# Rotary embedding: whole input resident on chip, loads queued first, 16 KB runs per partition, and a sine table in fewer steps

## The chip, the cores and the metric

The kernel runs on one core of a Trainium2 chip. The metric is device time in microseconds (us) of one execution. VectorE is called DVE, ScalarE ACT, GpSimd POOL and SyncE SP, as in the profile. The 16 DMA engines of the core move data between HBM and the on-chip memory (128 partitions). A DMA is issued by one of the engines' queues; those of POOL make one queue of their own (q0 in the profile), those of SP and ACT another kind (q1).

## The reference

`x` has 8 x 8 heads of 1024 positions with 64 features in f32 (16.8 MB); the output has the same shape and type. Each half of the features is rotated against the other by an angle that depends on the position and the feature:

```python
angles = np.outer(positions, freqs)          # 1024 x 32
cos, sin = np.cos(angles), np.sin(angles)
x_first, x_second = x[..., :half], x[..., half:]
out_first = x_first * cos - x_second * sin
out_second = x_first * sin + x_second * cos
```

## The kernel before

The positions are split over the 128 partitions: a partition owns 8 neighbouring positions (Q = 8) of every head. The sine and cosine tables are then 8 x 32 = 256 values per partition and serve all heads; they are repeated over the heads by a broadcast pattern.

The program first loads the frequencies (line 39, on POOL's queue) and the positions (line 44, on SP's), multiplies them (line 49) and adds a quarter turn for the cosine (line 52). Each of the two angle arrays is then reduced twice to one turn, on DVE (lines 58 to 65: scale, round by conversion to int32 and back, scale, subtract), ACT takes the sine of it (line 66), and DVE turns the result into bf16 (lines 71, 72).

The main loop (line 80) has eight tiles of K = 8 heads. A tile is a load from f32 in HBM to bf16 on chip (line 87), six bf16 operations on DVE with 2048 elements per partition each (lines 96 to 101: two products with the sine, two with the cosine, a difference, a sum), and a store from bf16 to f32 (line 102). Loads and stores are all issued by POOL, since they convert the type on the way. In HBM, a partition's part of one head is 512 floats, 2 KB in one run; a tile has eight such runs per partition, one per head, and neighbouring partitions lie 2 KB apart.

Input, output and the two temporaries t1 and t2 come from a pool of four buffers per name. A load of tile 4 or later therefore waits until DVE has read tile t - 4. Program order on each engine is laid down by the framework, which may put instructions of several tiles between one another; each engine works through its own instructions in order, and waits on semaphores for the others.

Of the kernel before, what the change touches and what calls it, by code (L numbers as in the profile page):

```python
# [2 lines left out]

# [4 lines left out]


@with_exitstack
def kernel(
    ctx: ExitStack,
    tc: tile.TileContext,
    x: bass.AP,
    freqs: bass.AP,
    positions: bass.AP,
    out: bass.AP,
):
    nc = tc.nc  # L20
    Sin = mybir.ActivationFunctionType.Sin

    b, h, seq, d = x.shape
    bh = b * h
    half = d // 2
    P = 128
    twopi = 2 * math.pi

    ss = d
    sbh = seq * d  # L30
    Q = seq // P
    assert Q * P == seq

    singles = ctx.enter_context(tc.tile_pool(name="singles", bufs=1))
    cspool = ctx.enter_context(tc.tile_pool(name="cs", bufs=1))
    pool = ctx.enter_context(tc.tile_pool(name="main", bufs=4))

    fr = singles.tile([P, 1, half], mybir.dt.float32)
    nc.gpsimd.dma_start(out=fr, in_=freqs[None, None, :].to_broadcast([P, 1, half]))  # L39

    pos_i = singles.tile([P, Q, 1], positions.dtype)
    pos_ap = bass.AP(tensor=positions.tensor, offset=positions.offset,
                     ap=[[Q, P], [1, Q], [1, 1]])
    nc.sync.dma_start(out=pos_i, in_=pos_ap)
    pos_f = singles.tile([P, Q, 1], mybir.dt.float32)
    nc.vector.tensor_copy(out=pos_f, in_=pos_i.bitcast(mybir.dt.int32)[:, :, :1])  # L46

    angles = cspool.tile([P, Q, half], mybir.dt.float32)
    nc.vector.tensor_mul(out=angles, in0=pos_f.to_broadcast([P, Q, half]),  # L49
                         in1=fr.to_broadcast([P, Q, half]))  # L50
    anglesc = cspool.tile([P, Q, half], mybir.dt.float32)
    nc.vector.tensor_scalar_add(out=anglesc, in0=angles, scalar1=math.pi / 2)
    sin_p = cspool.tile([P, 1, Q, half], mybir.dt.float32)
    cos_p = cspool.tile([P, 1, Q, half], mybir.dt.float32)
    for a, dst in ((angles, sin_p), (anglesc, cos_p)):
        for shift in (0.0, math.pi):
            if shift:
                nc.vector.tensor_scalar_add(out=a, in0=a, scalar1=shift)  # L58
            bfrac = cspool.tile([P, Q, half], mybir.dt.float32)
            nc.vector.tensor_scalar_mul(out=bfrac, in0=a, scalar1=1.0 / twopi)  # L60
            bint = cspool.tile([P, Q, half], mybir.dt.int32)
            nc.vector.tensor_copy(out=bint, in_=bfrac)  # L62
            nc.vector.tensor_copy(out=bfrac, in_=bint)  # L63
            nc.vector.tensor_scalar_mul(out=bfrac, in0=bfrac, scalar1=twopi)  # L64
            nc.vector.tensor_sub(out=a, in0=a, in1=bfrac)  # L65
        nc.scalar.activation(out=dst[:, 0, :, :], in_=a, func=Sin, scale=-1.0)  # L66

    bf16 = mybir.dt.bfloat16
    sin_h = cspool.tile([P, 1, Q, half], bf16)
    cos_h = cspool.tile([P, 1, Q, half], bf16)  # L70
    nc.vector.tensor_copy(out=sin_h, in_=sin_p)
    nc.vector.tensor_copy(out=cos_h, in_=cos_p)  # L72

    K = 8
    ntiles = bh // K
    sin_b = sin_h.to_broadcast([P, K, Q, half])
    cos_b = cos_h.to_broadcast([P, K, Q, half])
    sp = Q * ss

    for t in range(ntiles):  # L80
        g0 = t * K
        x_ap = bass.AP(tensor=x.tensor, offset=x.offset + g0 * sbh,
                       ap=[[sp, P], [sbh, K], [ss, Q], [1, d]])
        o_ap = bass.AP(tensor=out.tensor, offset=out.offset + g0 * sbh,
                       ap=[[sp, P], [sbh, K], [ss, Q], [1, d]])
        xt = pool.tile([P, K, Q, d], bf16)
        nc.gpsimd.dma_start(out=xt, in_=x_ap)  # L87
        ot = pool.tile([P, K, Q, d], bf16)
        of = ot[:, :, :, :half]
        os_ = ot[:, :, :, half:]  # L90
        t1 = pool.tile([P, K, Q, half], bf16)
        t2 = pool.tile([P, K, Q, half], bf16)
        xf = xt[:, :, :, :half]
        xs = xt[:, :, :, half:]
        v = nc.vector
        v.tensor_mul(out=t1, in0=xf, in1=sin_b)  # L96
        v.tensor_mul(out=t2, in0=xs, in1=sin_b)  # L97
        v.tensor_mul(out=of, in0=xf, in1=cos_b)  # L98
        v.tensor_sub(out=of, in0=of, in1=t2)  # L99
        v.tensor_mul(out=os_, in0=xs, in1=cos_b)  # L100
        v.tensor_add(out=os_, in0=os_, in1=t1)  # L101
        nc.gpsimd.dma_start(out=o_ap, in_=ot)  # L102


# [1 line left out]
_INS = ['x', 'freqs', 'positions']  # L106
_OUTS = [((8, 8, 1024, 64), 'float32')]


# [23 lines left out]
```

## Time and profile before

| | us |
|---|---|
| median of 3 runs (100.31 to 100.55) | 100.53 |
| span of the profiled execution, first to last instruction | 98.8 |
| what the median has beside that span | 1.73 |
| DVE busy | 62.8 |
| POOL busy, nearly all of it issuing DMAs | 15.0 |
| ACT busy | 2.1 |
| TensorE | not used |

The whole time of the profiled execution is not listed apart from its span, so the span stands for it and the third row of the table links it to the runs. In the profile's rows, `L96 DVE ... t<-xt,sin_h` is line 96 on DVE, writing t from xt and sin_h; what stands in brackets at the end of a row of the timeline is the time for which the engine stood idle before it, and what released it. In the groups by line, the two figures after the bar are the busy time of the group in us and the mean of one in ns. The engines' busy time in a DMA row can be over 1.00 of a stretch, because recorded packets of one DMA engine overlap. The rate in GB/s counts what a transfer writes: a load writes bf16, a store writes f32.

### The profile page before, as it was taken

To read this page: it belongs to the slowest core of one execution; us is meant where nothing else is said; L and a number is where in the kernel's file an instruction comes from. 1 tells how busy PE (TensorE), PEld (TensorE's weight loads), DVE (VectorE), ACT (ScalarE), POOL (GpSimd) and SP (SyncE) were. 2 spreads that over 40 slices of the span, in tenths; PEclk is the share of its full clock that TensorE was granted. 3 is DMA by queue.
4 is the path that set the end of the run, shared out by engine and by line. 5 is a ranking of instruction groups with operands and counts; after the bars stand their busy time and mean duration, and the time that the engine had idled before them with its cause. 6 is when DMAs were issued, how large, how long until landed. Compare 5 with 4: busy or idle time off the path is not lost.

```text
span 98.8 us, 150 instructions
## 1 busy us (share of the span) xinstructions
DVE 62.8 (64%) x75; ACT 2.1 (2%) x3; POOL 15.0 (15%) x21
## 2 busy tenths in 40 slices
DVE  0179973746999999999993000001999999991000
ACT  5000100010000000000000000000000000000000
POOL 5920000000033030302004900000002003003000
DMA  0699999999808999999999999999999997994992
GB/s 3 40 97 189 203 209 206 208 206 206 136 4 101 180 201 417 418 417 412 418 416 413 415 417 365 251 206 207 208 207 208 297 423 202 352 378 122 392 382 73
DMA packets 16817, 25.20 MB, mean 255 GB/s; under 512 B 416, under 2 KB 8624, under 8 KB 16816
## 3 DMA queue, kind: packets, MB, share of 16 engines
q0 software_dynamic: 16672, 25.18, 116.3%
q1 hardware_dynamic: 144, 0.01, 0.1%
q14 instruction: 1, 0.01, 0.0%
HBM read 16.80 MB, written 16.78 MB: 340 GB/s over the span
## 4 chain that ended last, share of the span: by engine, by line
issue 33%; DVE 30%; DMA 19%; POOL 7%; POOLq 1%; PEldq 0%
DMA xt<-in_x_dram 19%; DVE ot L101 6%; DVE ot L100 6%; DVE ot L99 6%; DVE ot L98 6%; POOL xt L87 4%; DVE t L96 4%; DVE t L97 3%; POOL out_dram L102 3%; POOLq L128 1%; POOL fr L39 1%; DVE cos_h L72 0%; POOLq L102 0%; PEldq L128 0%
## 5 line engine op out<-in xcount | busy, mean ns | idle before, releaser
L96 DVE TENSOR_TENSOR t<-xt,sin_h 128x2048 bf16<-128x2048 bf16 x8 | 9.8, 1220 | 20.9 <-DMA xt<-in_x_dram 20.9
L102 POOL DMA_DIRECT2D out_dram<-ot x8 | 7.1, 883 | 52.0 <-DVE ot L101 52.0
L87 POOL DMA_DIRECT2D xt<-in_x_dram x8 | 7.1, 898 | 22.6 <-DVE ot L100 22.6
L97 DVE TENSOR_TENSOR t<-xt,sin_h 128x2048 bf16<-128x2048 bf16 x8 | 9.7, 1217 | 0.0
L100 DVE TENSOR_TENSOR ot<-xt,cos_h 128x2048 bf16<-128x2048 bf16 x8 | 9.7, 1216 | 0.0
L98 DVE TENSOR_TENSOR ot<-xt,cos_h 128x2048 bf16<-128x2048 bf16 x8 | 9.7, 1216 | 0.0
L99 DVE TENSOR_TENSOR ot<-ot,t 128x2048 bf16<-128x2048 bf16 x8 | 9.7, 1215 | 0.0
L101 DVE TENSOR_TENSOR ot<-ot,t 128x2048 bf16<-128x2048 bf16 x8 | 9.7, 1215 | 0.0
L46 DVE CAST pos_f<-pos_i 128x8 f32<-128x8 int32 x1 | 0.4, 369 | 2.5 <-DMA pos_i<-in_positions_dram 2.5
L49 DVE TENSOR_TENSOR angles<-pos_f,fr 128x256 f32<-128x256 f32 x1 | 0.4, 424 | 2.4 <-DMA fr<-in_freqs_dram 2.4
L66 ACT ACT_TABLE_LOAD x1 | 1.3, 1283 | 0.7 <-PEq L117 0.7
L64 DVE TENSOR_SCALAR bfrac<-bfrac 128x256 f32<-128x256 f32 x4 | 1.2, 292 | 0.1
L62 DVE CAST bint<-bfrac 128x256 int32<-128x256 f32 x4 | 1.2, 292 | 0.1
L63 DVE CAST bfrac<-bint 128x256 f32<-128x256 int32 x4 | 1.2, 292 | 0.1
L65 DVE TENSOR_TENSOR angles<-angles,bfrac 128x256 f32<-128x256 f32 x2 | 0.8, 425 | 0.1
L65 DVE TENSOR_TENSOR anglesc<-anglesc,bfrac 128x256 f32<-128x256 f32 x2 | 0.8, 420 | 0.0
L39 POOL DMA_DIRECT2D fr<-in_freqs_dram x1 | 0.7, 706 | 0.8 <-PEq L128 0.8
L66 ACT ACTIVATE cos_p<-anglesc 128x256 f32<-128x256 f32 x1 | 0.4, 416 | 10.6 <-DVE anglesc L65 10.6
L60 DVE TENSOR_SCALAR bfrac<-anglesc 128x256 f32<-128x256 f32 x2 | 0.6, 290 | 0.0
L60 DVE TENSOR_SCALAR bfrac<-angles 128x256 f32<-128x256 f32 x2 | 0.6, 289 | 0.0
L66 ACT ACTIVATE sin_p<-angles 128x256 f32<-128x256 f32 x1 | 0.4, 416 | 7.8 <-DVE angles L65 7.8
L58 DVE TENSOR_SCALAR anglesc<-anglesc 128x256 f32<-128x256 f32 x1 | 0.3, 294 | 0.0
(8 smaller groups left out, 1.6 us busy)
## 6 DMA issues: line engine op xcount, KB each, us to landing
out_dram<-ot POOLq DMA_DIRECT2D x8, 2048.0 KB, 11.4
xt<-in_x_dram POOLq DMA_DIRECT2D x8, 1024.0 KB, 17.0
pos_i<-in_positions_dram SPq DMA_DIRECT2D x1, 8.0 KB, 1.8
fr<-in_freqs_dram POOLq DMA_DIRECT2D x1, 16.0 KB, 3.9
```

The source lines that it names most:

```text
L39: nc.gpsimd.dma_start(out=fr, in_=freqs[None, None, :].to_broadcast([P, 1, half]))
L60: nc.vector.tensor_scalar_mul(out=bfrac, in0=a, scalar1=1.0 / twopi)
L65: nc.vector.tensor_sub(out=a, in0=a, in1=bfrac)
L66: nc.scalar.activation(out=dst[:, 0, :, :], in_=a, func=Sin, scale=-1.0)
L87: nc.gpsimd.dma_start(out=xt, in_=x_ap)
L96: v.tensor_mul(out=t1, in0=xf, in1=sin_b)
L97: v.tensor_mul(out=t2, in0=xs, in1=sin_b)
L98: v.tensor_mul(out=of, in0=xf, in1=cos_b)
L99: v.tensor_sub(out=of, in0=of, in1=t2)
L100: v.tensor_mul(out=os_, in0=xs, in1=cos_b)
L101: v.tensor_add(out=os_, in0=os_, in1=t1)
L102: nc.gpsimd.dma_start(out=o_ap, in_=ot)
```

## The change

A partition now owns 64 neighbouring positions (C = 64) of one head: 16 partitions cover a head (`chunks`), a tile is 8 heads (`group`), and a tile in HBM is one unbroken piece of 2 MB in which each partition has one run of 64 x 64 floats, 16 KB. There are again eight tiles, and the six operations on each have the same sizes as before. The table is now 64 x 32 = 2048 values per partition, the same values in every 16th partition, without a broadcast over heads.

Input and output tiles have eight buffers each, so none is used twice; the temporaries have two. All eight loads stand in the program ahead of the table's computation. The positions are loaded by eight small DMAs, alternately from SP and ACT; the frequencies follow on ACT.

The table is computed in turns instead of radians: frequency divided by a full turn, product with the positions, rounding to whole turns by adding and subtracting a large constant in one instruction, one subtraction. ACT takes the sine of the remaining fraction and, for the cosine, the sine of a quarter turn less its absolute value, writing bf16 directly.

```diff
-    pool = ctx.enter_context(tc.tile_pool(name="main", bufs=4))
+    xpool = ctx.enter_context(tc.tile_pool(name="xin", bufs=ntiles))
+    opool = ctx.enter_context(tc.tile_pool(name="xout", bufs=ntiles))
+    tpool = ctx.enter_context(tc.tile_pool(name="tmp", bufs=2))
-    nc.gpsimd.dma_start(out=fr, in_=freqs[None, None, :].to_broadcast([P, 1, half]))
-    nc.sync.dma_start(out=pos_i, in_=pos_ap)
+    def hbm(t, g):
+        return bass.AP(tensor=t.tensor, offset=t.offset + g * P * run, ap=[[run, P], [1, run]])
+    for g in range(group):
+        eng = nc.sync if g % 2 == 0 else nc.scalar
+        eng.dma_start(
+            out=pos_i[g * chunks:(g + 1) * chunks],
...
+    nc.scalar.dma_start(out=fr, in_=freqs[None, :].to_broadcast([P, half]))
+    for g in range(ntiles):
+        xt = xpool.tile([P, C, d], bf16)
+        nc.gpsimd.dma_start(out=xt.rearrange("p c d -> p (c d)"), in_=hbm(x, g))
+        xts.append(xt)
...
+    nc.vector.tensor_scalar_mul(out=fturn[:, 0, :], in0=fr, scalar1=1.0 / twopi)
+    nc.vector.tensor_mul(out=turns, in0=pos_f.to_broadcast([P, C, half]),
+                         in1=fturn.to_broadcast([P, C, half]))
+    nc.vector.tensor_scalar(out=whole, in0=turns, scalar1=magic, scalar2=magic,
+                            op0=Alu.add, op1=Alu.subtract)
+    nc.vector.tensor_sub(out=turns, in0=turns, in1=whole)
+    nc.scalar.activation(out=sin_h, in_=turns, func=Sin, scale=twopi)
+    nc.scalar.activation(out=whole, in_=turns, func=mybir.ActivationFunctionType.Abs)
+    nc.scalar.activation(out=cos_h, in_=whole, func=Sin, scale=-twopi, bias=half_pi)
...
-        xt = pool.tile([P, K, Q, d], bf16)
-        nc.gpsimd.dma_start(out=xt, in_=x_ap)
-        nc.gpsimd.dma_start(out=o_ap, in_=ot)
+        nc.gpsimd.dma_start(out=hbm(out, g), in_=ot.rearrange("p c d -> p (c d)"))
```

On POOL, the whole queue of DMAs before, from the frequencies to the last store, in program order (xt is an input tile, ot an output tile):

```order
L39 DMA fr<-in_freqs_dram 128x32
L87 DMA xt<-in_x_dram 128x8x512 x5
L102 DMA out_dram<-ot 128x8x512 x5
L87 DMA xt<-in_x_dram 128x8x512 x3
L102 DMA out_dram<-ot 128x8x512 x3
```

And the same place on POOL now, from the end of the program's preamble:

```order
L118 MEMSET const-bfloat16-1.0 128x1
L118 MEMSET const-uint8-127 128x1
L129 UNCONDITIONAL_BRANCH
L62 DMA xt<-in_x_dram 128x4096 x8
L103 DMA out_dram<-ot 128x4096 x8
```

The frequencies have left this queue, the three loads that stood behind five stores have moved ahead of all stores, and each DMA's pattern has one run of 4096 elements per partition instead of eight of 512.

On DVE before, from the bf16 sine table to the first product with the cosine; the operations on 128x256 are the rest of the cosine table:

```order
L71 CAST sin_h<-sin_p 128x256
L60 TENSOR_SCALAR bfrac<-anglesc 128x256
L96 TENSOR_TENSOR t_115<-xt,sin_h 128x2048
L62 CAST bint<-bfrac 128x256
L97 TENSOR_TENSOR t_116<-xt,sin_h 128x2048
L63 CAST bfrac<-bint 128x256
L96 TENSOR_TENSOR t_127<-xt,sin_h 128x2048
L64 TENSOR_SCALAR bfrac<-bfrac 128x256
L97 TENSOR_TENSOR t_128<-xt,sin_h 128x2048
L65 TENSOR_TENSOR anglesc<-anglesc,bfrac 128x256
L96 TENSOR_TENSOR t_139<-xt,sin_h 128x2048
L72 CAST cos_h<-cos_p 128x256
```

On DVE now, from the start of the program to the first product with the cosine:

```order
L67 MEMSET half_pi 128x1
L69 CAST pos_f<-pos_i 128x64
L71 TENSOR_SCALAR fturn<-fr 128x32
L73 TENSOR_TENSOR turns<-pos_f,fturn 128x2048
L77 TENSOR_SCALAR whole<-turns 128x2048
L79 TENSOR_TENSOR turns<-turns,whole 128x2048
L97 TENSOR_TENSOR t_111<-xt,sin_h 128x2048
L98 TENSOR_TENSOR t_112<-xt,sin_h 128x2048
L97 TENSOR_TENSOR t_121<-xt,sin_h 128x2048
L98 TENSOR_TENSOR t_122<-xt,sin_h 128x2048
L99 TENSOR_TENSOR ot<-xt,cos_h 128x64x32
```

The table's operations stand ahead of all products instead of between those of tiles 0 to 2, and the sine products of two tiles, instead of three, stand ahead of the first cosine product.

More of the change, by code (lines that the diff above doesn't have):

```diff
@@ L20 @@
     nc = tc.nc
+    f32 = mybir.dt.float32
+    bf16 = mybir.dt.bfloat16
     Sin = mybir.ActivationFunctionType.Sin
+    Alu = mybir.AluOpType
     b, h, seq, d = x.shape
@@ L27 @@
     twopi = 2 * math.pi
[L29 to L32, printed above, removed]
-    singles = ctx.enter_context(tc.tile_pool(name="singles", bufs=1))
-    cspool = ctx.enter_context(tc.tile_pool(name="cs", bufs=1))
-    pool = ctx.enter_context(tc.tile_pool(name="main", bufs=4))
[L38 to L43, printed above, removed]
@@ L44 @@
-    nc.sync.dma_start(out=pos_i, in_=pos_ap)
-    pos_f = singles.tile([P, Q, 1], mybir.dt.float32)
-    nc.vector.tensor_copy(out=pos_f, in_=pos_i.bitcast(mybir.dt.int32)[:, :, :1])
[L48 to L85, printed above, removed]
-        xt = pool.tile([P, K, Q, d], bf16)
[L87 to L98, printed above, removed]
@@ new lines @@
+    C = 64
+    chunks = seq // C
+    group = P // chunks
+    ntiles = bh // group
+    run = C * d
+    assert chunks * C == seq and group * chunks == P and ntiles * group == bh
+    singles = ctx.enter_context(tc.tile_pool(name="singles", bufs=1))
+    xpool = ctx.enter_context(tc.tile_pool(name="xin", bufs=ntiles))
[3 more added lines that the diff above has]
+        return bass.AP(tensor=t.tensor, offset=t.offset + g * P * run, ap=[[run, P], [1, run]])
@@ new lines @@
+    pos_i = singles.tile([P, C, 1], positions.dtype)
+    for g in range(group):
+        eng = nc.sync if g % 2 == 0 else nc.scalar
+        eng.dma_start(
+            out=pos_i[g * chunks:(g + 1) * chunks],
+            in_=bass.AP(tensor=positions.tensor, offset=positions.offset,
+                        ap=[[C, chunks], [1, C], [1, 1]]))
+    fr = singles.tile([P, half], f32)
+    nc.scalar.dma_start(out=fr, in_=freqs[None, :].to_broadcast([P, half]))
+    xts = []
+    for g in range(ntiles):
+        xt = xpool.tile([P, C, d], bf16)
+        nc.gpsimd.dma_start(out=xt.rearrange("p c d -> p (c d)"), in_=hbm(x, g))
+        xts.append(xt)
@@ new lines @@
+    half_pi = singles.tile([P, 1], f32)
+    nc.vector.memset(half_pi, math.pi / 2)
+    pos_f = singles.tile([P, C, 1], f32)
+    nc.vector.tensor_copy(out=pos_f, in_=pos_i.bitcast(mybir.dt.int32)[:, :, :1])
+    fturn = singles.tile([P, 1, half], f32)
+    nc.vector.tensor_scalar_mul(out=fturn[:, 0, :], in0=fr, scalar1=1.0 / twopi)
+    turns = singles.tile([P, C, half], f32)
+    nc.vector.tensor_mul(out=turns, in0=pos_f.to_broadcast([P, C, half]),
+                         in1=fturn.to_broadcast([P, C, half]))
@@ new lines @@
+    whole = singles.tile([P, C, half], f32)
+    magic = 1.5 * 2.0 ** 23
+    nc.vector.tensor_scalar(out=whole, in0=turns, scalar1=magic, scalar2=magic,
+                            op0=Alu.add, op1=Alu.subtract)
+    nc.vector.tensor_sub(out=turns, in0=turns, in1=whole)
+    sin_h = singles.tile([P, C, half], bf16)
+    cos_h = singles.tile([P, C, half], bf16)
+    nc.scalar.activation(out=sin_h, in_=turns, func=Sin, scale=twopi)
+    nc.scalar.activation(out=whole, in_=turns, func=mybir.ActivationFunctionType.Abs)
@@ new lines @@
+    nc.scalar.activation(out=cos_h, in_=whole, func=Sin, scale=-twopi, bias=half_pi)
+    v = nc.vector
+    for g in range(ntiles):
+        xt = xts[g]
+        xf = xt[:, :, :half]
+        xs = xt[:, :, half:]
+        ot = opool.tile([P, C, d], bf16)
+        of = ot[:, :, :half]
+        os_ = ot[:, :, half:]
+        t1 = tpool.tile([P, C, half], bf16)
+        t2 = tpool.tile([P, C, half], bf16)
+        v.tensor_mul(out=t1, in0=xf, in1=sin_h)
+        v.tensor_mul(out=t2, in0=xs, in1=sin_h)
+        v.tensor_mul(out=of, in0=xf, in1=cos_h)
+        v.tensor_mul(out=os_, in0=xs, in1=cos_h)
@@ L99 @@
         v.tensor_sub(out=of, in0=of, in1=t2)
-        v.tensor_mul(out=os_, in0=xs, in1=cos_b)
         v.tensor_add(out=os_, in0=os_, in1=t1)
-        nc.gpsimd.dma_start(out=o_ap, in_=ot)
+        nc.gpsimd.dma_start(out=hbm(out, g), in_=ot.rearrange("p c d -> p (c d)"))
 _INS = ['x', 'freqs', 'positions']
```

## The prediction, on record before the changed kernel was run

> **What bounds the kernel now.** I read the whole span first, by slices, then the DMA rates of single stretches, then the waits, and only then the instructions. The page's two DMA rows say how full the transfers keep the 16 DMA engines; the issue rows say how long a transfer takes to land.
>
> ```profile
> span 98.8 us, 150 instructions
> DMA  0699999999808999999999999999999997994992
> GB/s 3 40 97 189 203 209 206 208 206 206 136 4 101 180 201 417 418 417 412 418 416 413 415 417 365 251 206 207 208 207 208 297 423 202 352 378 122 392 382 73
> q0 software_dynamic: 16672, 25.18, 116.3%
> HBM read 16.80 MB, written 16.78 MB: 340 GB/s over the span
> out_dram<-ot POOLq DMA_DIRECT2D x8, 2048.0 KB, 11.4
> xt<-in_x_dram POOLq DMA_DIRECT2D x8, 1024.0 KB, 17.0
> ```
>
> The engines are busy almost everywhere, and the rate has two steady levels. A load counts by what it writes on chip (1024 KB in bf16, from 2048 KB of f32 in HBM), so 206 GB/s of a load is 412 GB/s of HBM traffic, nearly the 416 of a store. Windows give the levels and the places where they are not reached (columns: stretch, length, busy us and instruction count of DVE, ACT and POOL, clock, DMA share, GB/s):
>
> ```profile
> 0.00:2.50 2.50, 0.00 (x0) 1.28 (x1) 1.41 (x6) 1.00 0.03 3
> 2.50:7.50 5.00, 2.41 (x8) 0.00 (x0) 3.03 (x4) 1.00 0.83 71
> 7.50:10.00 2.50, 2.26 (x8) 0.18 (x1) 0.00 (x0) 1.00 1.19 193
> 10.00:25.00 15.00, 9.80 (x19) 0.65 (x2) 0.00 (x0) 1.00 1.24 206
> 25.00:26.00 1.00, 1.00 (x2) 0.00 (x0) 0.00 (x0) 1.00 1.17 195
> 26.00:29.00 3.00, 3.00 (x4) 0.00 (x0) 0.88 (x1) 1.00 0.18 29
> 29.00:34.00 5.00, 5.00 (x5) 0.00 (x0) 0.88 (x1) 1.00 0.87 121
> 34.00:36.00 2.00, 2.00 (x3) 0.00 (x0) 0.88 (x1) 1.00 1.11 155
> 38.00:58.00 20.00, 14.79 (x14) 0.00 (x0) 5.27 (x6) 1.00 1.47 416
> ```
>
> One load at 206 GB/s takes 1.0486 MB / 206 = 5.09 us, one store at 416 takes 2.0972 MB / 416 = 5.04 us: eight of each are 81.0 us of steady transfer. The span has 17.8 us more. Up to 10 us the engines moved 0.85 MB, worth 4.1 us, so the start costs 5.9. From 25 to 36 us they moved 1.20 MB, worth 5.8 of 11 us: 5.2 lost. The rest, some 6.7, lies near the end. Who made them wait is in the timeline:
>
> ```profile
> 0.74 0.37 SPq L44 DMA_DIRECT2D pos_i<-in_positions_dram  x1
> 1.29 0.71 POOL L39 DMA_DIRECT2D fr<-in_freqs_dram  x1 [0.85 <-PEq L128]
> 1.99 3.53 POOL L87 DMA_DIRECT2D xt<-in_x_dram  x4
> 5.29 0.42 DVE L49 TENSOR_TENSOR angles<-pos_f,fr 128x256 f32<-128x256 f32 x1 [2.39 <-DMA fr<-in_freqs_dram]
> 12.97 1.23 DVE L96 TENSOR_TENSOR t<-xt,sin_h 128x2048 bf16<-128x2048 bf16 x1 [0.68 <-DMA xt<-in_x_dram]
> 28.11 0.88 POOL L87 DMA_DIRECT2D xt<-in_x_dram  x1 [22.58 <-DVE ot L100]
> 53.95 2.65 POOL L87 DMA_DIRECT2D xt<-in_x_dram  x3
> 68.69 1.22 DVE L96 TENSOR_TENSOR t<-xt,sin_h 128x2048 bf16<-128x2048 bf16 x1 [15.90 <-DMA xt<-in_x_dram]
> 88.00 1.21 DVE L101 TENSOR_TENSOR ot<-ot,t 128x2048 bf16<-128x2048 bf16 x1
> 89.82 0.89 POOL L102 DMA_DIRECT2D out_dram<-ot  x1 [6.24 <-DVE ot L101]
> ```
>
> With four input buffers the fifth load had to wait 22.58 us until DVE freed one; the queue ran dry from 26 to 29 us. Loads 6 to 8 were issued at 53.95, behind five stores, so DVE stood still for 15.90 us until 68.69 and then had three tiles left, each with a store to follow: the queue ran dry between these stores, and the last one was issued at 89.82. So **the bound is the DMA queue, and about 10 us are lost because DVE and the queue wait for each other in turn**. DVE's own main work is 48 multiplies and adds, spaced (88.00 - 68.69) / 17 = 1.136 us, 54.5 us in all: shorter than the transfers.
>
> **The change part by part.** *All eight loads first, no buffer reuse.* POOL has nothing ahead of the loads now (the frequencies moved to ACT's queue), so the first goes out at 1.29 instead of 1.99. All eight are in the queue by 1.29 + 8 x 0.88 = 8.3 us at the old issue cost; the queue needs the second only when the first is through. Stores queue behind the loads. No load waits for DVE any more, so the queue never runs dry if each store is issued before its turn, and the span becomes: first load's issue, its landing, fifteen transfers, the end. What is late next is the queue itself.
>
> *First landing.* The trace has two loads that started on an empty queue.
>
> ```profile
> DMA to landing us min/median/max: 9.8/17.0/23.4
> DMA to landing us min/median/max: 7.8/11.4/13.9
> ```
>
> The first row is of the loads, the second of the stores. The load at 28.11 took the 9.8; the first one 12.97 - 1.99 = 10.98, the highest bound. A store on an empty queue took 7.8 (the last), the lowest. What slowed the first load, the frequencies ahead of it or cold reads, no row separates. I take the middle of the two loads, 10.35.
>
> *Longer runs.* A packet of before is 2 KB on the HBM side: 16 x 2048 B / 416 GB/s = 78.8 ns apart on each engine. The new runs are 16 KB, eight packets in one. No row shows such packets. At one end nothing is gained and the rate stays 416. At the other end, the smallest packets tell what a packet can cost by itself; this is the stretch up to 2.2 us, in which only the positions travel:
>
> ```profile
> DMA packets 144, 0.01 MB, mean 4 GB/s; under 512 B 144, under 2 KB 144, under 8 KB 144
> q1 hardware_dynamic: 144, 0.01, 3.9%
> ```
>
> That is 0.039 x 16 x 2.2 us / 144 = 9.5 ns a packet of some 57 B. A straight line from (57 B, 9.5 ns) to (2048 B, 78.8 ns) leaves 7.5 ns fixed. Saving seven of them in eight packets (52 of 630 ns) gives 453 GB/s. The recorded times of packets overlap (share 1.47 at full rate), so 7.5 is too much; I take the middle of the ends, 434 GB/s: 4.83 us a tile instead of 5.09, fifteen further transfers 72.5 us.
>
> The Trainium skill ("DMA: Bandwidth & Descriptors", "Why small descriptors are slow (HBM only)") charges each packet about 3 cycles beside one cycle per 32 B. That makes 67 cycles of a 2 KB packet and 515 instead of 536 for eight in one, 4% less: the estimate by it would be 433 GB/s and the same total, against 90.5 us if the trace's rate stays.
>
> *The sum.* First landing 1.29 + 10.35 - 0.26 (the first tile's own gain) = 11.4; fifteen more, 72.5: last landing at 83.9. From the last landing before (89.82 + 7.8 = 97.6) to the end of the span were 1.2 us: 85.1. The median of 100.53 stands 1.73 above the profiled span of 98.8, which I keep: **86.8 us**.
>
> *The sine table* is covered. It shrinks from 26 DVE operations on 256 elements to three large ones on 2048 per partition (a product, a rounding, a subtraction) and three activations; the old ones are:
>
> ```profile
> L64 DVE TENSOR_SCALAR bfrac<-bfrac 128x256 f32<-128x256 f32 x4 | 1.2, 292 | 0.1
> L65 DVE TENSOR_TENSOR angles<-angles,bfrac 128x256 f32<-128x256 f32 x2 | 0.8, 425 | 0.1
> L66 ACT ACTIVATE sin_p<-angles 128x256 f32<-128x256 f32 x1 | 0.4, 416 | 7.8 <-DVE angles L65 7.8
> pos_i<-in_positions_dram SPq DMA_DIRECT2D x1, 8.0 KB, 1.8
> fr<-in_freqs_dram POOLq DMA_DIRECT2D x1, 16.0 KB, 3.9
> ```
>
> At most eight times their duration: 3.4 + 2.3 + 3.4 us on DVE and 3.3 for each activation. At least, the 1.2 us of a 2048-element bf16 operation for each. The inputs: SP and ACT issue four position loads each (0.74 + 4 x 0.37 = 2.2), the frequency load behind them on ACT waits for one to land (0.74 + 1.8), is out at 2.9 and lands at 4.7 with the 1.8 us of the positions, at 6.8 with its own 3.9 of before. With some 0.4 us of small DVE work, sin is ready by 19.6 at the latest and by 10 at the earliest. ACT's table load (1.28 in the first window) stands behind its DMA issues and is done long before.
>
> DVE then does tile 0's and tile 1's sine products before any cosine product. Tile 1 lands at 11.4 + 4.8 = 16.2; I take sin ready before it, cos two activations later but behind four DVE products, so DVE runs on from 16.2 with 46 operations: 16.2 + 46 x 1.136 = 68.5. At the latest values (sin 19.6, cos 26.2, then 44 operations) it ends at 76.2. The last landing stands at 83.9 in the sum, and a store on an empty queue lands 7.8 after its issue, so DVE has time until 76.1. So the table and the new waits cost nothing; the loads and early stores hide them. If that cover were gone, each us of DVE delay would be one of span.
>
> *Order of the adds, separate output buffers, the bf16 table straight from ACT*: same 48 DVE operations, no wait on the path; nothing.
>
> **The rivals.** *No gain from longer runs.* For it: loads of 1 KB and stores of 2 KB on chip have the same spacing, so the packet may be limited by HBM. Then 1.29 + 10.35 + 7 x 5.09 + 8 x 5.04 + 1.2 + 1.73 = **90.5 us** (91.1 with the slow first landing).
>
> *The new address pattern slows the DMA* (the case on the other side). Before, neighbouring partitions read 2 KB apart; now 16 KB apart, so engines working in step could fall on the same part of HBM. For it: the trace shows packets that are slow while the engines are full, 121 and 155 GB/s with shares of 0.87 and 1.11 between 29 and 36 us. Against it: a tile is one unbroken 2 MB piece now, and 207 and 416 are steady elsewhere. If loads ran at 155 throughout, they would take 6.77 us each; with stores slowed alike (416 x 155 / 206 = 313, 6.70 us), first landing 13.3, then 7 x 6.77 + 8 x 6.70 = 101.0, total **117 us**; with loads alone slowed, 104. It turns slower than before from 5.69 us a tile on average (369 GB/s of HBM traffic): (100.53 - 1.73 - 1.2 - 1.29 - 10.35 + 5.09) / 16.
>
> [...]
>
> *DVE comes late* (a table that takes longer than the bounds, or loads and stores that interleave so that tiles 6 and 7 land late). Were DVE to end at 80, the end would be 80 + 7.8 + 1.2 + 1.73 = **90.7 us**.
>
> *The loads aren't really all queued ahead*: if the queue took only five before blocking, as before, stores would stand between them; POOL issued four in 3.53 us without a stall and three behind stores, so nothing shows a limit. It would cost up to the 5 us of one dry spell: 92.
>
> **How the numbers follow.** Forecast 86.8: 0.60. No gain, 90.5: 0.22. DVE late or loads not all ahead, 90.7 to 92: 0.07. Slow pattern, 104 to 117: 0.09; something between, 0.02. The unknown costs, each at its end with the other at its value: 453 GB/s gives 83.5; a first landing of 7.8 gives 84.3; no gain with 10.98 gives 91.1. One dip like that of 34 to 36 us (2 us at 155 instead of 206) is 0.5 us more. Range **83.5 to 92.0**, leaving out the slow pattern. Differences within 0.3% count as no change, about what a measurement can tell here: faster 0.90, same 0.01, slower 0.09.
>
> **What would show it.** In the changed profile the GB/s row should hold one level near 215 for some 39 us and then one near 430 without a hole; a hole refutes the queue argument, 206 and 416 the packet gain, less the pitch. The first product on tile 1 should start near 16 us, the last addition near 68.5, and the last store should wait in the queue about 15 us from issue to landing. DVE ending after 76 would make it the bound. The first landing tells the start's term.

## The result and the profile after

The changed kernel takes 87.23 us (median of 4 runs, 87.08 to 87.44) against 100.42 for the kernel before on the same chip: ratio 0.8674, 95% interval 0.8646 to 0.8702. The forecast was 86.8, range 83.5 to 92.0. The profiled execution took 87.28, with a span of 85.5.

From the page of the changed kernel: busy time, DMA by 40 slices (2.1 us each now), the load queue's total, and the issues with their size and median time to landing.

```profile
span 85.5 us, 146 instructions
DVE 60.8 (71%) x54; ACT 7.0 (8%) x4; POOL 8.8 (10%) x20
DMA  0799979999999999999999999999999999999990
GB/s 8 81 225 208 184 140 231 203 226 203 226 203 226 211 218 215 215 222 207 222 326 460 399 475 391 475 391 475 383 475 391 468 391 468 391 468 368 376 368 0
q0 software_dynamic: 2304, 25.17, 96.4%
out_dram<-ot POOLq DMA_DIRECT2D x8, 2048.0 KB, 13.2
xt<-in_x_dram POOLq DMA_DIRECT2D x8, 1024.0 KB, 24.4
fr<-in_freqs_dram ACTq DMA_DIRECT2D x1, 16.0 KB, 11.7
```

The holes are gone: one level for the loads, one for the stores. Of the slices in mid-stream one stays low, 140 GB/s at 11 to 13 us. The queue moved the same 25 MB in 2304 packets instead of 16672. A slice of 2.1 us holds three to four packets of 0.61 us per engine (the spacing is worked out in the table below); that may be why the slices alternate between 391 and 475, which was not looked into. And one row doesn't fit the forecast: the frequencies took 11.7 us to land, not 3.9.

The timeline of the changed kernel at the places that the prediction spoke of (start, duration, engine, line; in brackets the idle time before it and what ended it):

```profile
1.25 4.37 POOL L62 DMA_DIRECT2D xt<-in_x_dram  x8 [0.81 <-PEq L129]
2.60 0.43 ACTq L56 DMA_DIRECT2D fr<-in_freqs_dram  x1
8.60 0.20 DVE L69 CAST pos_f<-pos_i 128x64 f32<-128x64 int32 x1 [7.73 <-DMA pos_i<-in_positions_dram]
14.31 0.18 DVE L71 TENSOR_SCALAR fturn<-fr 128x32 f32<-128x32 f32 x1 [5.52 <-DMA fr<-in_freqs_dram]
20.44 1.91 ACT L82 ACTIVATE sin_h<-turns 128x2048 bf16<-128x2048 f32 x1 [16.09 <-DVE turns L79]
22.38 1.22 DVE L97 TENSOR_TENSOR t<-xt,sin_h 128x2048 bf16<-128x2048 bf16 x1 [1.98 <-ACT sin_h L82]
24.66 1.22 DVE L97 TENSOR_TENSOR t<-xt,sin_h 128x2048 bf16<-128x2048 bf16 x1
75.73 1.24 DVE L102 TENSOR_TENSOR ot<-ot,t 128x2048 bf16<-128x2048 bf16 x1
77.27 0.53 POOL L103 DMA_DIRECT2D out_dram<-ot  x1 [6.28 <-DVE ot L102]
```

DVE was free from 8.80 until the frequencies came at 14.31. Its first product on tile 0 started at 22.38, and the first one on tile 1 at 24.66 instead of 16.2. Its last addition ended at 76.97, not 68.5. The time to landing, first of the loads' view and then of the stores':

```profile
DMA to landing us min/median/max: 8.2/24.4/39.7
DMA to landing us min/median/max: 6.5/13.2/18.1
```

And its windows (columns as in the prediction): the low stretch of the loads, called the dip below, the rate behind it, and the steady level of the stores.

```profile
9.00:12.50 3.50, 0.00 (x0) 0.00 (x0) 0.00 (x0) 1.00 0.82 155
12.50:16.00 3.50, 1.65 (x2) 0.00 (x0) 0.00 (x0) 1.00 1.03 211
55.00:75.00 20.00, 20.00 (x19) 0.00 (x0) 1.59 (x3) 1.00 1.06 431
```

So the first load landed at 1.25 + 8.2 = 9.45 and the last store, the one with the shortest time, at 77.27 + 6.5 = 83.77. The prediction wanted some 15 us from issue to landing there; 6.5 is also the shortest time in the run with a later table below, so the queue had next to nothing left in front of that store: DVE's end came too late for it.

### The profile page after: what moved, and what is told of

The parts are those of the page before. It is cut to its first block, busy times and chain, and to the rows that moved or that the text cites. A ratio compares the mean times of both kernels' runs of the same rounds, so it can differ in the third digit from the quotient of the medians.

```text
span 85.5 us, 146 instructions
## 1 busy us (share of the span) xinstructions
DVE 60.8 (71%) x54; ACT 7.0 (8%) x4; POOL 8.8 (10%) x20
## 3 DMA queue, kind: packets, MB, share of 16 engines
q0 software_dynamic: 2304, 25.17, 96.4%
## 4 chain that ended last, share of the span: by engine, by line
issue 75%; DMA 10%; POOL 4%; POOLq 1%; PEldq 0%
DMA xt<-in_x_dram 10%; POOL out_dram L103 4%; POOLq L129 1%; POOLq L103 0%; PEldq L129 0%
## 5 line engine op out<-in xcount | busy, mean ns | idle before, releaser
L103 POOL DMA_DIRECT2D out_dram<-ot x8 | 4.3, 533 | 67.9 <-DVE ot L102 67.9
L62 POOL DMA_DIRECT2D xt<-in_x_dram x8 | 4.4, 579 | 0.8 <-PEq L129 0.8
L82 ACT ACTIVATE sin_h<-turns 128x2048 bf16<-128x2048 f32 x1 | 1.9, 1909 | 16.1 <-DVE turns L79 16.1
L79 DVE TENSOR_TENSOR turns<-turns,whole 128x2048 f32<-128x2048 f32 x1 | 2.3, 2293 | 0.0
L73 DVE TENSOR_TENSOR turns<-pos_f,fturn 128x2048 f32<-128x2048 f32 x1 | 2.3, 2293 | 0.0
L85 ACT ACTIVATE cos_h<-whole,half_pi 128x2048 bf16<-128x2048 f32 x1 | 2.0, 2002 | 0.0
L84 ACT ACTIVATE whole<-turns 128x2048 f32<-128x2048 f32 x1 | 1.9, 1893 | 0.0
L77 DVE TENSOR_SCALAR whole<-turns 128x2048 f32<-128x2048 f32 x1 | 1.2, 1227 | 0.0
## 6 DMA issues: line engine op xcount, KB each, us to landing
fr<-in_freqs_dram ACTq DMA_DIRECT2D x1, 16.0 KB, 11.7
```

Of the source, the lines that this page charges most:

```text
L62: nc.gpsimd.dma_start(out=xt.rearrange("p c d -> p (c d)"), in_=hbm(x, g))
L73: nc.vector.tensor_mul(out=turns, in0=pos_f.to_broadcast([P, C, half]), in1=fturn.to_broadcast([P, C, half]))
L79: nc.vector.tensor_sub(out=turns, in0=turns, in1=whole)
L82: nc.scalar.activation(out=sin_h, in_=turns, func=Sin, scale=twopi)
L85: nc.scalar.activation(out=cos_h, in_=whole, func=Sin, scale=-twopi, bias=half_pi)
L103: nc.gpsimd.dma_start(out=hbm(out, g), in_=ot.rearrange("p c d -> p (c d)"))
```

## The experiments

Times are medians; ratios are to the kernel before, run beside each experiment (100.5 to 100.6 us), with their 95% intervals. The question of the first four was which part of the change brings the 13 us: the order of the loads, the longer runs, or the table.

### Loads first, all else as before

```diff
-    pool = ctx.enter_context(tc.tile_pool(name="main", bufs=4))
+    pool = ctx.enter_context(tc.tile_pool(name="main", bufs=8))
...
+    for t in range(ntiles):
+        x_ap = bass.AP(tensor=x.tensor, offset=x.offset + t * K * sbh,
+                       ap=[[sp, P], [sbh, K], [ss, Q], [1, d]])
+        xt = pool.tile([P, K, Q, d], bf16)
+        nc.gpsimd.dma_start(out=xt, in_=x_ap)
+        xts.append(xt)
     angles = cspool.tile([P, Q, half], mybir.dt.float32)
...
-        xt = pool.tile([P, K, Q, d], bf16)
-        nc.gpsimd.dma_start(out=xt, in_=x_ap)
+        xt = xts[t]
```

> The kernel before (2 KB runs, old table, frequencies on POOL's queue), with eight buffers and all loads issued ahead of everything else. Theory (the gain is two sums: no dry spells, about 9 us, and longer runs, about 3 us): the first tile lands at 13.0 as before, fifteen transfers of 5.07 follow without a hole, and 1.2 to 2.1 of end: 91.9 to 92.9 us. Rival (the longer runs bring most of it): 96 to 100. Rival (the shorter table brings part of it): above 94, with DVE's last addition late enough to leave a hole before the last store.

Measured: 91.52 us, ratio 0.9109 (0.9081 to 0.9138). The DMA rows of its page:

```profile
DMA  0589999999999999999999999999999999999990
GB/s 4 24 76 188 205 207 208 206 208 207 207 206 209 206 207 208 207 209 205 207 276 415 419 414 416 413 417 414 415 414 416 415 415 413 418 416 414 416 277 13
```

There is no hole from 10 us on, and the rates are those of before. The order of the loads, with the eight buffers that it needs, brings 9.0 us alone, with the old table and the short runs. Both rivals expected a longer time. The time is 0.4 us below the range that I had expected.

### The changed kernel with short runs

```diff
-    C = 64
+    C = 8
+    R = 64 // C
...
-        return bass.AP(tensor=t.tensor, offset=t.offset + g * P * run, ap=[[run, P], [1, run]])
+        return bass.AP(tensor=t.tensor, offset=t.offset + g * R * P * run,
+                       ap=[[run, P], [P * run, R], [1, run]])
...
```

The other lines of the diff give the tiles the dimension R and repeat the smaller table over it by a broadcast.

> The changed kernel with 8 positions per partition again, so runs of 2 KB; loads first and the short table stay (on 256 elements). Theory: 5.07 us a tile, 15 x (5.07 - 4.87) = 3.0 us more than the changed kernel, less what the first landing changes. If the frequencies ahead of the loads in POOL's queue had made the first landing late (13.0 before, 9.4 after), it stays near 9.6 here and the time is 90 us or less; if the short runs had, it is near 12.2 and the time 91 to 92. Rival (the table matters): over 1 us faster than the kernel before with loads first, beyond the difference of the two first landings. The frequencies, 11.7 us from issue to landing in the changed kernel, should land in under 5 us here, if they waited behind 16 KB packets.

Measured: 91.11 us, ratio 0.9060 (0.9026 to 0.9093). The time to landing of its loads:

```profile
DMA to landing us min/median/max: 10.8/25.4/40.1
```

Its timeline where the frequencies arrive:

```profile
3.59 0.45 DVE L73 TENSOR_SCALAR fturn<-fr 128x32 f32<-128x32 f32 x1 [1.11 <-DMA fr<-in_freqs_dram]
```

And its windows of the early loads and the steady stores:

```profile
9.00:12.50 3.50, 0.34 (x1) 0.00 (x0) 0.00 (x0) 1.00 1.14 164
55.00:75.00 20.00, 11.75 (x11) 0.00 (x0) 1.76 (x2) 1.00 1.47 415
```

The first tile lands at 1.27 + 10.8 = 12.1 although nothing stands ahead of the loads in POOL's queue; with loads first and the frequencies ahead of them it also took 10.8 from its issue. So the frequencies had not made the start slow. With runs of 16 KB the first tile lands at 9.45. The time is only 0.4 us below that of the kernel before with loads first, and the first landing is 0.7 earlier: so the short table brings nothing that can be seen. The frequencies were here in 3.6 us; they were also issued first here, since one DMA is enough for the positions, so this alone doesn't show that long packets delay them. The loads have a dip here too, 164 GB/s, without packets of another queue beside them; its cause stays open.

### Long runs without the order

The changed kernel with its loads back in the loop and four buffers (diff: `bufs=ntiles` becomes `bufs=4`, also `bufs=2` of the temporaries, and the load moves to where `xts[g]` was read).

> The changed kernel with loads issued in the loop and four buffers for input and output; 16 KB runs and the short table stay. POOL's order is again five loads, five stores, three loads, three stores. Theory: the dry spells return, only the rate stays: 16 x 0.2 = 3 us and about 2 us at the start below the kernel before, 94 to 98 us, with holes in the GB/s row. Rival (longer runs bring most of it): 87 to 90.

Measured: 99.04 us, ratio 0.9846 (0.9826 to 0.9867). The rates of its page:

```profile
GB/s 13 119 218 206 144 200 212 216 216 212 3 0 51 175 165 324 432 432 432 432 432 432 432 256 432 378 216 216 216 216 216 270 432 324 357 445 61 432 432 0
```

Its timeline at loads 6 to 8 and at DVE's first operation on tile 5:

```profile
57.29 1.60 POOL L85 DMA_DIRECT2D xt<-in_x_dram  x3
68.12 1.23 DVE L93 TENSOR_TENSOR t<-xt,sin_h 128x2048 bf16<-128x2048 bf16 x1 [11.64 <-DMA xt<-in_x_dram]
```

The holes are back, at rates of 216 and 432. It came out a us above the range: I had counted 5 us for rate and start, and had not counted that the table was late here as well (DVE's first sine product at 22.3), so the three loads behind the stores were issued at 57.29 instead of 53.95. Here, where DVE and the queue wait for each other, most of what the faster transfers gained went into longer waits.

### Runs of 4 KB

The same edit as for the short runs, with `C = 16`.

> The changed kernel with 16 positions per partition, so runs of 4 KB. Theory (a fixed part in each packet): a straight line through 78.9 ns at 2 KB and 608 ns at 16 KB has 3.3 ns fixed, so 154.5 ns at 4 KB and 4.94 us a tile, 1.2 us more than the changed kernel over fifteen tiles: 88 to 88.8 us. Rival (the gain needs long runs, through another mechanism than a fixed part): as with 2 KB runs, 5.06 us a tile, 90 us.

Measured: 88.99 us, ratio 0.8845 (0.8827 to 0.8864). Its window of steady stores:

```profile
55.00:75.00 20.00, 11.28 (x10) 0.00 (x0) 1.49 (x2) 1.00 1.24 424
```

Its early loads, and the time to landing of all of them:

```profile
9.00:12.50 3.50, 1.93 (x3) 1.87 (x3) 0.00 (x0) 1.00 1.12 211
DMA to landing us min/median/max: 10.3/24.9/39.7
```

The window of steady stores with runs of 8 KB, from the last experiment below:

```profile
55.00:75.00 20.00, 9.40 (x9) 0.00 (x0) 1.43 (x2) 1.00 1.12 429
```

| run in HBM | GB/s | packet spacing on an engine, 16 x bytes / rate | fixed part against 2 KB |
|---|---|---|---|
| 2 KB | 415 | 79.0 ns | |
| 4 KB | 424 | 154.6 ns | 2 x 79.0 - 154.6 = 3.4 ns |
| 8 KB | 429 | 305.5 ns | (4 x 79.0 - 305.5) / 3 = 3.5 ns |
| 16 KB | 431 | 608.2 ns | (8 x 79.0 - 608.2) / 7 = 3.4 ns |

Three lengths give the same fixed part, so the rate follows it. The time missed the expected range by only 0.2 us, and that is luck: the first tile lands at 11.6 here, 2.1 later than in the changed kernel, which the expectation left out. It also left out that the loads have no dip (211 GB/s) and that DVE ends early, which by the figures further below took back some 1.3 of it.

### The frequencies first

The second question was the end: DVE's last addition had come 8 us later than predicted, without much harm as it seemed, and the loads had dipped while the frequencies' packets ran.

```diff
+    fr = singles.tile([P, half], f32)
+    nc.sync.dma_start(out=fr, in_=freqs[None, :].to_broadcast([P, half]))
     pos_i = singles.tile([P, C, 1], positions.dtype)
...
-    fr = singles.tile([P, half], f32)
-    nc.scalar.dma_start(out=fr, in_=freqs[None, :].to_broadcast([P, half]))
```

> The changed kernel with the frequency load first on SP's queue instead of last on ACT's. In the changed kernel its packets ran between load packets from 8.2 to 13 us, where the loads fell from 211 to 155 GB/s (9.0 to 12.5 us, 0.9 us of transfer), and DVE got the frequencies at 14.3 us. Theory (the small packets themselves disturb the loads, and DVE's end at 77 us is level with the queue): the frequencies land before 5 us, DVE starts its table when the positions are there (8.6), ends near 71.3, the loads have no dip, 1.0 to 1.3 us less: 85.9 to 86.3. Rival (the dip belongs to the loads, as the one at 10 us with 2 KB runs and early frequencies): only DVE gets earlier, 87.0 to 87.2.

Measured: 86.05 us (85.91 to 86.21), ratio 0.8551 (0.8529 to 0.8572), below that of the changed kernel (0.8674, and 0.8685 with 0.8663 to 0.8707 when it was run again). Its timeline at the table's inputs and at the last store:

```profile
3.85 0.20 DVE L71 TENSOR_SCALAR fturn<-fr 128x32 f32<-128x32 f32 x1 [2.98 <-DMA fr<-in_freqs_dram]
9.73 0.20 DVE L69 CAST pos_f<-pos_i 128x64 f32<-128x64 int32 x1 [5.69 <-DMA pos_i<-in_positions_dram]
72.70 0.53 POOL L103 DMA_DIRECT2D out_dram<-ot  x1 [6.28 <-DVE ot L102]
```

Its stores' time to landing, and behind it the window of the dip:

```profile
DMA to landing us min/median/max: 10.0/16.8/21.7
```

```profile
9.00:12.50 3.50, 2.70 (x3) 0.00 (x0) 0.00 (x0) 1.00 1.04 218
```

The dip is gone (218 GB/s against 155), DVE works from the landing of the positions (at 9.73, not the 8.6 that I had taken), and the last store waits 10.0 us in the queue instead of 6.5. This is the fastest version of the study.

### A later table, with late and with early frequencies

```diff
     nc.vector.tensor_sub(out=turns, in0=turns, in1=whole)
+    for _ in range(1):
+        nc.vector.tensor_add(out=turns, in0=turns, in1=whole)
+        nc.vector.tensor_sub(out=turns, in0=turns, in1=whole)
```

In the changed kernel:

> The changed kernel with two more f32 operations on DVE in the table's chain (add and subtract the whole turns again), 2.29 us each, so everything on DVE is 4.6 us later. Theory (DVE's last addition stands level with the queue: last store issued at 77.3, the queue free for it at 78): nothing is hidden, 91.5 to 91.9 us. Rival (as predicted blind, 7 us of cover remain): 87.2 to 87.5.

Measured: 91.50 us, ratio 0.9097 (0.9076 to 0.9118). With the frequencies first:

> Both: frequencies first, and the two more DVE operations. Theory: DVE ends near 71.3 + 4.6 = 75.9, so the same delay is hidden here: within 0.3 us of the kernel with the frequencies first alone. Rival (DVE's chain sets the end in any case): 4.6 us more than that one.

Measured: 87.36 us, ratio 0.8679 (0.8661 to 0.8698). The last store in the timeline, with late frequencies and then with early ones:

```profile
81.76 0.53 POOL L106 DMA_DIRECT2D out_dram<-ot  x1 [6.28 <-DVE ot L105]
```

```profile
77.13 0.53 POOL L106 DMA_DIRECT2D out_dram<-ot  x1 [6.28 <-DVE ot L105]
```

The stores' time to landing, in the same order:

```profile
DMA to landing us min/median/max: 6.5/8.9/13.4
```

```profile
DMA to landing us min/median/max: 7.0/12.5/17.4
```

In the changed kernel the delay of 4.5 us costs 4.3: no cover is left. With the frequencies first it costs 1.3, more than the 0.3 that I allowed. The positions land late there (9.5 to 9.7, not the 8.6 that I had taken), so DVE's end was 76.8, not 75.9. The rows then agree: with the frequencies first the last store landed at 72.70 + 10.0 = 82.70, and a store takes 6.5 to 7.0 at least, so it must be issued by 75.7 to 76.2; 77.13 is 0.9 to 1.4 too late.

### Only DVE earlier

To part the dip from DVE's lateness, the changed kernel with late frequencies and a shorter table. It leaves out the reduction to one turn and scales the sine by a small number instead, so the table's values are others.

```diff
-    nc.vector.tensor_scalar(out=whole, in0=turns, scalar1=magic, scalar2=magic,
-                            op0=Alu.add, op1=Alu.subtract)
-    nc.vector.tensor_sub(out=turns, in0=turns, in1=whole)
...
-    nc.scalar.activation(out=sin_h, in_=turns, func=Sin, scale=twopi)
+    nc.scalar.activation(out=sin_h, in_=turns, func=Sin, scale=0.005)
...
-    nc.scalar.activation(out=cos_h, in_=whole, func=Sin, scale=-twopi, bias=half_pi)
+    nc.scalar.activation(out=cos_h, in_=whole, func=Sin, scale=-0.005, bias=half_pi)
```

> The changed kernel without the rounding to whole turns and the subtraction, and with a smaller factor in the sine, so DVE starts on the tiles 3.6 us earlier while the frequencies stay where they are; the table's values are left wrong by it. Theory (of the 1.2 us that the frequencies-first kernel gained, some 0.9 is the dip of the loads and only 0.1 to 0.3 is DVE): 86.8 to 87.1 us, with the dip at 9 to 12.5 us still there (about 155 GB/s). Rival (DVE's lateness is all of it): 86.0 to 86.2.

Measured: 86.92 us (86.83 to 87.07), ratio 0.8644 (0.8626 to 0.8663); the changed kernel, run again, took 87.33 (87.12 to 87.73), as expected of it:

> The changed kernel as it is, beside the one with the shorter table on the same chip: 87.1 to 87.4 us.

The window of the dip with the shorter table, and the last store in its timeline:

```profile
9.00:12.50 3.50, 0.00 (x0) 0.00 (x0) 0.00 (x0) 1.00 0.83 152
```

```profile
73.62 0.53 POOL L100 DMA_DIRECT2D out_dram<-ot  x1 [6.28 <-DVE ot L99]
```

The dip is still there, the last store is issued 3.7 us earlier, and 0.3 to 0.4 us is gained. The other 0.9 of what the early frequencies bring is about the size of the dip: 3.5 us x (1 - 155 / 211) = 0.93. It is a net figure: between the first and the last landing the version with early frequencies saves 1.3 us against this one, and its first load lands some 0.5 us later. The other traces with runs of 8 or 16 KB agree: with late frequencies the same window has 152 to 159 GB/s (long runs without the order, the later table, the changed kernel run again), with early ones 208 (the later table) and 217 (8 KB).

### Runs of 8 KB with the frequencies first

The edit of the short runs with `C = 32`, and the frequencies moved.

> Frequencies first, and 32 positions per partition: runs of 8 KB. Theory (3.3 ns fixed in a packet): 305.6 ns a packet, 4.89 us a tile against 4.87, 0.4 us over fifteen tiles, less up to 0.3 us at the start: 0 to 0.5 us more than the kernel with frequencies first at 16 KB. Rival (short packets ramp up more slowly, as 2 and 4 KB did): 1 us more.

Measured: 86.59 us (86.50 to 86.72), ratio 0.8608 (0.8589 to 0.8628): 0.54 us above the 16 KB version, just past the 0.5 that was expected. The rate accounts for 15 x (2.097 / 429 - 2.097 / 431) = 0.34 of it. The time to landing of its loads:

```profile
DMA to landing us min/median/max: 8.5/23.0/37.7
```

## Why the prediction was right, and where it was not

| term | predicted | measured |
|---|---|---|
| first load's issue and landing | 11.4 | 9.45 |
| fifteen further transfers | 72.5 | 83.77 - 9.45 = 74.3 |
| last landing to end of span | 1.2 | 85.5 - 83.77 = 1.7 |
| beside the span | 1.73 | 87.28 - 85.5 = 1.8 |
| sum | 86.8 | 87.28 (the profiled execution; the median is 87.23) |

**The bound and the rival of the unchanged rate.** That the DMA queue sets the time, and that DVE and the queue waiting for each other in turn cost about 10 us, was right: loads first alone brought 9.0. The rival without a gain from longer runs (90.5 to 91.1) is what the short runs measured, 91.11. One reason given for it was a misreading: in the kernel before, a packet of a store is 1 KB on chip, since the output tile is bf16, and 2 KB in HBM, just like that of a load. Their equal spacing therefore says nothing about which side limits a packet.

**Longer runs.** The value taken, 434 GB/s, was right within 1%: 431 was measured, 4.87 us a tile instead of 4.83, which is 0.5 us of the 1.8 that the second term was short. The fixed part of a packet is 3.4 ns; the bound of 7.5 from the smallest packets was twice that. That its half fits is luck in part, since the middle of two ends was taken without a row for it. The Trainium skill's price of some 3 cycles a packet ("DMA: Bandwidth & Descriptors", "Why small descriptors are slow (HBM only)") gave an estimate of 433 GB/s, and the trace, with 431, agrees.

**First landing.** This term was mis-sized by 2.0 us. (The middle of the two old landings would be 10.39; 10.35 is a slip of no weight.) The frequencies were not the cause. The landing goes with the run length: 10.8 us from issue at 2 KB, 10.3 at 4 KB, 8.5 at 8 KB, 8.1 to 8.7 at 16 KB. POOL's issue time and the number of position loads change along with it, and no run parts these, so why longer runs land earlier stays open.

**The sine table is covered.** This is the step that failed: "So the table and the new waits cost nothing; the loads and early stores hide them." It rested on the frequencies landing at 6.8 us at the latest, "with its own 3.9 of before". They were moved to the end of ACT's queue, behind four position loads, and came at 14.3; between 8 and 14.5 us the trace has 142 small packets of that queue among 157 load packets of 0.6 us. Whether the length of those packets or the place behind the position loads held the frequencies up was not parted; issued before the stream, they took 3.1 us. The table itself took 8.0 us from the frequencies to the sine (14.31 to 22.35) and not the 12.8 allowed, so the whole delay is that of the frequencies. DVE's end moved from 68.5 to 77.0, past the 76.1 that the prediction itself named, and nothing of the 7.6 us of cover between the two was left, as the later table showed (4.3 of 4.5 us paid). The prediction's own latest values ended at 76.2 and had no cover either, so "cost nothing" did not follow from them. Being late cost 0.3 to 0.4 us by DVE, and the dip of the loads, which the sum had no term for, another 0.9: together the remaining 1.3 of the second term. The rival "DVE comes late", held unlikely, thus came true in part.

That the total came out within half a percent is luck: the early first landing (-2.0) stood against the dip, the late DVE, the rate (+1.8 together) and the end (+0.5). The first three of these were not foreseen.

**Slower by the address pattern** did not happen: 431 GB/s is above every steady rate of before. The loads were all queued ahead, in 4.37 us, faster than thought.

## What to carry to other kernels

Where a transfer queue and an engine release each other in turn, count the transfers at their steady rate first; if the sum is well under the span, taking the loads out of the cycle can be worth more than making each faster: here 9.0 us against 1.5 for longer runs, with the new table, that stay in the cycle. The longer runs paid more when the queue never ran dry: 3.9 us with the loads first (91.11 against 87.23). A small load that every tile depends on belongs ahead of the big loads in time, not only on another queue; and "covered by the stream" should be tested by adding delay, since cover can be used up without the time showing it.

## What was not expected of the hardware

A 16 KB load of frequencies, issued at 2.60, took 11.7 us beside load packets of 16 KB (0.6 us each on an engine), and 3.1 us when it was issued at 0.74, before the stream. With 4 KB runs, issued at 1.33, just behind the first load, it took 6.7. While it ran late beside 16 KB packets, the stream lost a quarter of its rate (155 against 211 GB/s). With 2 KB runs the loads had a similar dip (164 GB/s at 9 to 12.5 us) with the frequencies long landed, but the kernel before with loads first had none at the same rate; what made the one with 2 KB runs was not found, so small packets are not the only thing that can slow the loads there. POOL's issue of a load took 0.55 us (4.37 / 8) with 16 KB runs against 0.88 with 2 KB.
